# Retention scores cut to halves of 256 tokens, and a new order for the sampled states and the recurrence's chunks

## The chip, the core and the metric

The kernel runs on one core of one Trainium2 chip. The metric is the device time of one execution in microseconds (us). Engine names are those of the profile: PE is TensorE (PEld its weight loads), DVE is VectorE, ACT is ScalarE, POOL is GpSimd, and SP is the engine that mostly issues DMAs. Every engine works through its own instructions in a fixed order, and waits at the first one whose inputs are not there.

## What is computed

One layer of a decoder for a prompt of 512 tokens (D_MODEL 1024) and, beside it, for 8 sampled sequences of one token that continue from stored states. One input projection feeds two branches, retention (4 heads, key width 256, value width 512) and RWKV-7 (16 heads of 64). Both are gated, projected down, merged, projected out, and followed by a gated per-layer embedding and a final norm. The part that the change rewrites is the retention of one head:

```python
def chunk(s, qkv):
    qc, kc, vc = qkv
    inner = jnp.einsum('bhid,bhjd->bhij', qc, kc) * dmask
    o = jnp.einsum('bhij,bhjv->bhiv', inner, vc) + jnp.einsum('bhid,bhdv->bhiv', qc * q_dec, s)
    s = chunk_dec * s + jnp.einsum('bhjd,bhjv->bhdv', kc * k_dec, vc)
    return s, o
```

`dmask` is the decay to the power of the distance, lower triangular. The result does not depend on how long a chunk is: with one chunk of 512 there is no state term, with two of 256 the second half takes the first half's state. The outputs are the rows of both sets, the new retention and RWKV states of both, and the last normalised rows.

## The kernel before

All large products are made in a split form: an operand is written as a high part (a rounded copy, made by ACT) and a low part (the rest, made by DVE), and three matmuls stand for one. A weight block of 512 KB is fetched by SP into one of three `raw` buffers, ACT makes `whi` (line 147), DVE makes `wlo` (line 148), and PE runs the matmuls of line 160 on 128 x 128 weights with 256 or 264 columns of tokens (tokens 0 to 255, and 256 to 519, the last 8 of these being the sampled tokens). One projection of 128 output channels is 48 such matmuls.

The order of the instructions on each engine is made by a planner that simulates the program with a cost model and gives each engine the ready instruction of highest priority. Program order is the priority, `tc.high_priority(offset=n)` moves a block ahead of later code, and `tc.issue_after(x)` places the block's instructions on x's own engine behind x. `after(i, prior)` adds a real wait between two engines.

The stages, with their place in the profiled execution:

1. 0 to about 270 us: norm, transposes, and the inputs of RWKV (keys, receptances, values, gates), written to DRAM in the layout of the recurrence.
2. About 270 to 710 us: the loop over 4 heads of retention. Each head makes k and q (`rope`), then v in four blocks `j` of 256 input channels (line 838), the scores `sc` (line 863), the sampled sequences (`sampled(h)`: 4 MB of states in four tiles `tS` of 1 MB, loaded by POOL at line 758, decayed by ACT at line 764, updated by DVE at line 765, read by PE at line 770, stored by POOL at line 774), four gate projections, the outputs `o` (line 910), the new state `st` (line 921) and the transposes `ot` (line 928). The scores of key tile `jt` cover all later tokens: 512, 384, 256 and 128 columns, six matmuls each. The outputs of token tile `it` take 3(it+1) matmuls of 512 columns. Beside this DVE works off a triangular solve for RWKV and the sampled RWKV states in portions (`advance`).
3. About 700 to 900 us: `fills()`, which is eight projections `gate(O_MB, m)` of 48 matmuls and then eight `down_a(m)` of 96 matmuls (the fills, 16 in all), and beside them the eight steps `chunk(c)` of the RWKV recurrence. A chunk is a chain: PE `UO` (64 small matmuls, line 1025), copies `R` on ACT and DVE, PE `U` (line 1034), copies into `SV`, PE `dS` (line 1040) and `UO` (line 1043), DVE the next `SV` (line 1049), ACT `Ot` (line 1056). The banks of UO are two, so the next chunk's UO also waits for `Ot`. After each second chunk follow `finish_rwkv` (DVE and ACT) and `emit_rwkv` (PE transposes `gt`, line 985, and DVE). The list `AT` says after how many fills each chunk stands in the program. All chunks have high priority, so that the planner may run them ahead of that place.
4. After the last chunk: `emit_rwkv` of the last pair, PE transposes `so` of the last state (line 1133), then the RWKV rows `yb` are loaded back (line 1149; the first load waits for the transposes), split into `ybhi` and `yblo` (lines 1150 and 1151), and projected by `w_down_b`. That projection is the next PE work behind the fills.
5. About 900 us to the end: `w_down_b`, `w_out`, the embedding and the output.

Of the kernel before, what the change touches and what calls it, by code (L numbers as in the profile page):

```python
# [41 lines left out]
def constants():  # L42
    import numpy as np

    f = np.float32
    c = {}
    inv = (10000.0 ** (-np.arange(128) / 128)).astype(f)
    pos = np.concatenate([np.arange(T), np.full(B8, 4096)]).astype(f)
    ang = (pos[:, None] * inv[None, :]).astype(f)
    c["cos"] = np.ascontiguousarray(np.cos(ang).T.astype(f))  # L50
    c["sin"] = np.ascontiguousarray(np.sin(ang).T.astype(f))
    j = np.arange(128)[:, None]
    i = np.arange(T)[None, :]
    c["dmask"] = np.stack([np.where(i >= j, GAM[h] ** np.maximum(i - j, 0) / 16.0, 0.0) for h in range(H)], 1).astype(f)
    jj = np.arange(T).reshape(4, 128).T
    c["kdec"] = np.stack([GAM[h] ** (511 - jj) / 16.0 for h in range(H)], 1).astype(f)
    s = np.arange(64)[:, None]
    t = np.arange(64)[None, :]
    le, lt = (s <= t).astype(f), (s < t).astype(f)
    ev = np.concatenate([np.concatenate([le, -0.5 * lt], 1), np.concatenate([le, lt], 1)], 0)  # L60
    od = np.concatenate([np.concatenate([-0.5 * lt, le], 1), np.concatenate([lt, le], 1)], 0)
    c["gmask"] = np.concatenate([ev, od, ev, od], 1)
    r = np.ones((128, NT), f)
    r[:, 0:T:C] = 0.0
    r[:, T:] = 0.0
    c["reset"] = r
    ind = np.zeros((128, NPAIR, 16), f)
    for p in range(NPAIR):
        ind[:64, p, 2 * p] = 1.0
        ind[64:, p, 2 * p + 1] = 1.0  # L70
    c["ind"] = ind
    c["indT"] = np.ascontiguousarray(np.concatenate([ind.transpose(2, 1, 0)] * 2, 0))
    bd = np.zeros((128, 128), f)
    bd[:64, :64] = 1.0
    bd[64:, 64:] = 1.0
    c["bdiag"] = bd
    return c


def body(tc, A, O, dbg=None, upto="Z"):  # L80
# [11 lines left out]
    with es:  # L92
# [516 lines left out]
        pB.tile([128, 1280], F32R, tag="ihi", name="ihi")  # L609
# [135 lines left out]
        dve.tensor_tensor(s8, s8, i4[:, 2], ALU.add)  # L745
        dve.tensor_tensor(sum8, s8, i4[:, 3], ALU.add)

        def sampled(h):
            qz = pR.tile([128, 2, 4, 34], F32, tag="qz", name="qz", bufs=1)
            dve.memset(qz, 0.0)  # L750
            dve.tensor_copy(qz[:, :, :, 0], qs[:, h, :, 0:4])
            dve.tensor_copy(qz[:, :, :, 33], qs[:, h, :, 4:8])
            po = pq.tile([128, 512], F32, tag="po", name="po")
            for g in range(2):
                Ss = []
                for i in range(2):
                    S = pT.tile([128, 4, NT], F32, tag="tS", name="tS", bufs=4)[:, :, 0:DV]
                    pool.dma_start(S, A["state_ret"][0, 4 * g:4 * g + 4, h, 128 * i:128 * i + 128, :].rearrange("b p v -> p b v"))
                    Ss.append(S)
                for b in range(4):  # L760
                    vb = bank("vb")
                    pe.matmul(vb, sel[:, 4 * g + b, :], vsr, start=True, stop=True)  # L762
                    for i, S in enumerate(Ss):
                        act.activation(S[:, b, :], S[:, b, :], AF.Copy, scale=GAM[h])  # L764
# [26 lines left out]
        OFF = [0, 512, 896, 1152]  # L791
        GBC = [0, 0, 0, 4, 8]
        for h in range(H):
            roped = {}
# [32 lines left out]
            for j in range(4):  # L827
                ready = fetch(w_in[256 * j:256 * j + 256, O_V + DV * h:O_V + DV * h + DV])
                raws, w = raws[-1:] + [wide(ready[0])], [wide(t) for t in weights(None, ready=ready)]
                if j % 2:  # L830
                    ms = [pe.matmul(vsm[32 * g:32 * g + 32], hst[:, 2 * j - 2 + g, :], raws[g // 2][:, g % 2, :],  # L831
                                    start=(j == 1), stop=(j == 3), skip_group_check=True) for g in range(4)]
                    side_by_side(ms)
                    after(ms[0], marks[2])
                for jt in range(4):
                    for k in range(2):
                        for x, (w_, r) in enumerate(((w[0], hhi), (w[0], hlo), (w[1], hhi))):
                            m_ = pe.matmul(vps[jt], r[:, 2 * j + k, 128 * jt:128 * jt + 128], w_[:, k, :],  # L838
                                           start=(j == 0 and k == 0 and x == 0), stop=(j == 3 and k == 1 and x == 2))
                tail[:] = [getattr(m_, "ins", m_)]  # L840
                advance("v")
            vhi = pB.tile([128, 4, DV], F32R, tag="vhi", name="vhi")
            vlo = pB.tile([128, 4, DV], F32R, tag="vlo", name="vlo")
# [7 lines left out]
            qhi, qlo, _ = roped["q"]  # L851
            khi, klo, kf = roped["k"]

            dmask = pB.tile([128, T], F32, tag="dmask", name="dmask", bufs=1)
            (sp if h else pool).dma_start(dmask, A["dmask"][:, h, :])
            ihi = pB.tile([128, 1280], F32R, tag="ihi", name="ihi")
            ilo = pB.tile([128, 1280], F32R, tag="ilo", name="ilo")
            for jt in range(4):
                n = T - 128 * jt
                ps = bank("sc")  # L860
                seq = [(i, a_, b_) for i in range(2) for a_, b_ in ((khi, qhi), (khi, qlo), (klo, qhi))]
                for x, (i, a_, b_) in enumerate(seq):
                    pe.matmul(ps[:, 0:n], a_[:, i, 128 * jt:128 * jt + 128], b_[:, i, 128 * jt:T],  # L863
                              start=(x == 0), stop=(x == 5))
                s_ = pB.tile([128, T], F32, tag="s_", name="s_", bufs=1)
                dve.tensor_tensor(s_[:, 0:n], ps[:, 0:n], dmask[:, 0:n], ALU.mult)
# [12 lines left out]
            for jt in range(4):  # L879
# [5 lines left out]
            po = sampled(h)  # L885

            gs = []
            for i in range(4):
                g = pB.tile([128, NT], F32, tag="vg", name="gs", bufs=4)
                for (j, c0, c1), ps in zip(HV, proj(w_in[:, col(O_GA + DV * h, i)], hhi, hlo)):  # L890
                    act.activation(g[:, c0:c1], ps, AF.Silu)
                act.activation(gs8[:, 4 * h + i, :], g[:, T:NT], AF.Copy)
                gs.append(g)
                advance("gate")
                if h == H - 1 and i == 2:
                    ya_tiles(h, pT)
# [7 lines left out]
            ot = [x[:, i, :] for x in (pB.tile([128, 2, DV], F32, tag=t, name="ot") for t in ("qhi", "qlo")) for i in range(2)]  # L904
            for it in range(4):
# [5 lines left out]
                o = ot[it]  # L911
                act.activation(o, ps, AF.Square, accum_out=oss[:, it:it + 1])
                act.activation(o, ps, AF.Copy)
            rsqrt(ort, oss, 1.0 / DV, NORM_EPS)
            for it in range(4):
                act.activation(ot[it], ot[it], AF.Copy, scale=ort[:, it:it + 1])
            for i in range(2):
                ps = bank("st")
                seq = [(jt, a_, b_) for jt in range(4) for a_, b_ in ((dhi, vhi), (dhi, vlo), (dlo, vhi))]
                for x, (jt, a_, b_) in enumerate(seq):  # L920
                    pe.matmul(ps, a_[:, jt, 128 * i:128 * i + 128], b_[:, jt, :], start=(x == 0), stop=(x == 11))  # L921
# [408 lines left out]
```

## Time and profile before

| | |
|---|---|
| median of 3 runs | 1075.98 us (1072.61 to 1078.3) |
| profiled execution | 1071.51 us, its span 1069.7 us |
| PE / PEld busy | 1042.0 / 974.8 us |
| DVE / ACT / POOL busy | 785.2 / 494.8 / 79.5 us |
| mean granted PE clock | 0.992 |
| moved by DMA | 199.45 MB, mean 186 GB/s |

The span runs from the first to the last instruction. Matmuls overlap in their pipeline and their ends are modelled: the duration of one is longer than its distance to the next, and a PE that is shown busy is not a PE at its peak. A wait row names who waited, for whom, the total, the number of times and the longest.

### The profile page before, as it was taken

The page shows a single profiled execution, that of the slowest core. Times are in us where ns is not written, and L with a number is a line of the kernel's source. Part 1 is how long each engine was busy: PE and PEld are TensorE (multiplying, and loading weights), DVE is VectorE, ACT ScalarE, POOL GpSimd, SP SyncE. Part 2 cuts the span into 40 slices and gives each one's busy share as a digit, 9 for nine tenths or more (in the row PEclk, how much of TensorE's full clock was granted, in tenths as well). Part 3 has the DMA queues.
Part 4 walks back from the last instruction along what each step waited for, and adds up shares of the span by engine and source line. Part 5 has one row for each costly group of instructions (what it writes and reads, how often), then busy time and mean ns, then how long its engine had stood idle before and what let it go on. Part 6 is the DMA issues. An engine that isn't in the chain of part 4 may idle for free.

```text
span 1069.7 us, 22049 instructions
## 1 busy us (share of the span) xinstructions
PE 1042.0 (97%) x8932; PEld 974.8 (91%) x8932; DVE 785.2 (73%) x1429; ACT 494.8 (46%) x973; POOL 79.5 (7%) x139
## 2 busy tenths in 40 slices
PE   7999999999999999999999999998999999999995
PEld 6999989999879788987989889898999999999995
DVE  6647989884499699949894698864777755666875
ACT  6744565544464543373445333354323224334554
POOL 2000110100300200010010000110001100000000
PEclk8999999999999999999999999999999999999998
DMA  5623488788943943493288633969996649643222
GB/s 182 179 80 99 122 191 223 188 246 228 330 160 90 327 146 99 144 319 103 86 310 229 230 115 112 328 198 330 309 283 214 171 145 302 206 119 100 81 59 81
DMA packets 239224, 199.45 MB, mean 186 GB/s; under 512 B 58988, under 2 KB 203225, under 8 KB 237970
## 3 DMA queue, kind: packets, MB, share of 16 engines
q1 hardware_dynamic: 225586, 149.60, 47.7%
q0 software_dynamic: 13376, 48.17, 13.2%
q8 instruction: 70, 1.15, 0.4%
q14 instruction: 32, 0.26, 0.1%
q10 hardware_dynamic: 160, 0.27, 0.1%
HBM read 137.70 MB, written 60.00 MB: 185 GB/s over the span
## 4 chain that ended last, share of the span: by engine, by line
PE 85%; DMA 6%; DVE 3%; ACT 2%; issue 1%; SPq 1%; POOL 0%; DVEq 0%; POOLq 0%; ACTq 0%
PE ph L160 58%; PE phv L838 8%; PE o L910 3%; PE st L921 2%; PE sc L863 1%; PE po L770 1%; PE g L506 1%; PE UO L1025 1%; DMA raw<-in_w_ple_gate_dram 1%; DMA raw<-in_w_in_dram 1%; DMA yalo<-YAd 1%; DMA BKt<-BKd 1%; DMA MBd<-mg 1%; PE vb L762 1%; PE vsm L831 1%
## 5 line engine op out<-in xcount | busy, mean ns | idle before, releaser
L160 PE MATMUL ph<-hhi,whi 128*128 128x256 f32 (+2 forms) x1296 | 370.5, 286 | 0.9 <-ACT hhi L282 0.4
L160 PE MATMUL ph<-hlo,whi 128*128 128x256 f32 (+2 forms) x1296 | 369.4, 285 | 0.2 <-DVE hlo L283 0.2
L160 PE MATMUL ph<-hhi,wlo 128*128 128x256 f32 (+2 forms) x1296 | 368.8, 285 | 0.5 <-DVE wlo L148 0.5
L160 PEld LDWEIGHTS ph<-hhi,whi 128*128 128x128 f32 x1296 | 244.2, 189 | 6.1 <-issue 1.7
L160 PEld LDWEIGHTS ph<-hhi,wlo 128*128 128x128 f32 x1296 | 245.0, 189 | 2.2 <-DVE wlo L148 0.7
L160 PEld LDWEIGHTS ph<-hlo,whi 128*128 128x128 f32 x1296 | 244.5, 189 | 1.9 <-DVE hlo L283 0.7
L147 ACT ACTIVATE whi<-raw 128x1024 fp32r<-128x1024 f32 x135 | 142.9, 1059 | 208.9 <-PE ph L160 154.2
L148 DVE TENSOR_TENSOR wlo<-raw,whi 128x1024 fp32r<-128x1024 f32 x135 | 164.8, 1221 | 86.4 <-ACT whi L147 85.4
L160 PE MATMUL ph<-yalo,whi 128*128 128x256 f32 (+1 forms) x256 | 72.4, 285 | 0.0
L160 PE MATMUL ph<-yahi,whi 128*128 128x256 f32 (+1 forms) x256 | 72.2, 284 | 0.0
L160 PE MATMUL ph<-yahi,wlo 128*128 128x256 f32 (+1 forms) x256 | 71.9, 285 | 0.0
L623 DVE TENSOR_TENSOR tm<-M 128x62 f32<-128x62 f32 (+30 forms) x62 | 52.9, 853 | 0.6
L625 DVE TENSOR_TENSOR M<-M,tm 128x62 f32<-128x62 f32 (+30 forms) x62 | 52.8, 852 | 0.6
L838 PE MATMUL phv<-whi,hhi 128*128 128x512 f32 x128 | 51.5, 403 | 0.0
L838 PE MATMUL phv<-whi,hlo 128*128 128x512 f32 x128 | 50.5, 395 | 0.0
L160 PEld LDWEIGHTS ph<-yalo,whi 128*128 128x128 f32 x256 | 48.1, 188 | 0.3
L160 PEld LDWEIGHTS ph<-yahi,whi 128*128 128x128 f32 x256 | 48.1, 188 | 0.2
L160 PEld LDWEIGHTS ph<-yahi,wlo 128*128 128x128 f32 x256 | 47.8, 188 | 0.3
L838 PE MATMUL phv<-wlo,hhi 128*128 128x512 f32 x128 | 46.8, 395 | 0.5 <-DVE wlo L148 0.5
L765 DVE SCALAR_TENSOR_TENSOR tS<-vb,ks,tS 128x512 f32<-128x512 f32 x64 | 44.1, 742 | 3.3 <-PE vb L762 3.3
L764 ACT ACTIVATE tS<-tS 128x512 f32<-128x512 f32 x64 | 35.0, 620 | 12.5 <-DMA tS<-in_state_ret_dram 12.4
L215 ACT ACTIVATE mg<-ph 128x256 f32<-128x256 f32 (+1 forms) x48 | 17.7, 378 | 41.2 <-PE ph L160 20.6
(454 smaller groups left out, 2120.0 us busy)
## 6 DMA issues: line engine op xcount, KB each, us to landing
raw<-in_w_in_dram SPq DMA_DIRECT2D x97, 512.0 KB, 5.0
tS<-in_state_ret_dram POOLq DMA_DIRECT2D x16, 1024.0 KB, 8.4
out_dram<-tS POOLq DMA_DIRECT2D x16, 1024.0 KB, 9.9
KR<-KRd SPq DMA_DIRECT2D x8, 1024.0 KB, 9.5
raw<-in_w_down_a_dram SPq DMA_DIRECT2D x16, 512.0 KB, 6.8
KRd<-KRS SPq DMA_DIRECT2D x16, 256.0 KB, 4.5
KRd<-GM SPq DMA_DIRECT2D x16, 256.0 KB, 4.8
BKt<-BKd SPq DMA_DIRECT2D x8, 512.0 KB, 9.9
```

Of the source, the lines that this page charges most:

```text
L147: cp = act.activation(hi, raw, AF.Copy)
L148: sb = dve.tensor_tensor(lo, raw, hi, ALU.subtract)
L160: m_ = pe.matmul(ps[:, 0:c1 - c0], w[:, k, :], r[:, k0 + k, c0:c1], start=(x == 0), stop=(x == n_ - 1))
L215: act.activation(g[:, c0:c1], ps, fn, scale=scale)
L506: ms = [pe.matmul(gs[2 * q + hh][:, c * 128:(c + 1) * 128], BK[hs_, 4 * q + c, :], KRS[hs_, 4 * q + c, :], start=True, stop=True) for q in ...
L623: dve.tensor_tensor(tv, M[:, 0:s, s:s + 1].to_broadcast([128, s, n]), M[:, s:s + 1, s + 1:C].to_broadcast([128, s, n]), ALU.mult)
L625: dve.tensor_tensor(M[:, 0:s, s + 1:C], M[:, 0:s, s + 1:C], tv, ALU.add)
L764: act.activation(S[:, b, :], S[:, b, :], AF.Copy, scale=GAM[h])
L765: last = dve.scalar_tensor_tensor(S[:, b, :], vb, ks[:, h, i, 4 * g + b:4 * g + b + 1], S[:, b, :], ALU.mult, ALU.add)
L838: m_ = pe.matmul(vps[jt], r[:, 2 * j + k, 128 * jt:128 * jt + 128], w_[:, k, :], start=(j == 0 and k == 0 and x == 0), stop=(j == 3 and k ...
L910: pe.matmul(ps, a_[:, o_:o_ + 128], b_[:, jt, :], start=(x == 0), stop=(x == len(seq) - 1))
L921: pe.matmul(ps, a_[:, jt, 128 * i:128 * i + 128], b_[:, jt, :], start=(x == 0), stop=(x == 11))
```

## The change

Four edits are made together.

The scores are made within halves of 256 tokens: key tiles 0 to 3 cover 256, 128, 256 and 128 columns. The state of the first half is made from dhi and dlo (whose decay runs to token 511) and split into `shi` and `slo`; the outputs of token tiles 2 and 3 are the product of q with it (`oc`, six matmuls of 512 columns each), scaled per token by `qdec`, plus the scores of the second half. The state `st` at the end is then the second half's product plus `shi` plus `slo`, added by DVE.

The four loads of the sampled states of a head are issued in one go (`sampled_states`); in head 0 the first two wait for the last matmul of v's block 1, the other two for that of block 3 (`vmark`). The sampled work of head 0 moves behind the first gate projection.

In the recurrence, chunk c stands after 6, 8, 9, 10, 11, 12 and 13 fills for c = 1 to 7 (before: 3, 6, 8, 9, 11, 12 and 13), and its matmuls are now held behind the last matmul of those fills (`issue_after(tail[0])`).

```diff
+            SS = sampled_states(h)       # h == 0: after(ld, vmark[g]) on each load
+            if h:
+                po = sampled(h, SS)
...
-                n = T - 128 * jt
+                n = HT - 128 * (jt % 2)
...
+            vk = ((dhi, vhi), (dhi, vlo), (dlo, vhi))
+            shi = pB.tile([128, 2, DV], F32R, tag="shi", name="shi")
+            slo = [p_.tile([128, DV], F32R, tag=t, name="slo", bufs=1) for p_, t in ((pB, "vph"), (pR, "on"))]
+            for i in range(2):
+                ps = bank("st")
+                for x, (jt, (a_, b_)) in enumerate((jt, ab) for jt in range(2) for ab in vk):
+                    pe.matmul(ps, a_[:, jt, 128 * i:128 * i + 128], b_[:, jt, :], start=(x == 0), stop=(x == 5))
+                act.activation(shi[:, i, :], ps, AF.Copy)
+                dve.tensor_tensor(slo[i], ps, shi[:, i, :], ALU.subtract)
...
-                seq = [(jt, a_, b_) for jt in range(it + 1) for a_, b_ in ((ihi, vhi), (ihi, vlo), (ilo, vhi))]
+                seq = [(jt, a_, b_) for jt in range(it // 2 * 2, it + 1) for a_, b_ in ((ihi, vhi), (ihi, vlo), (ilo, vhi))]
...
+            ot = [pB.tile([128, NT], F32, tag="ro_k", name="ot", bufs=2)[:, 0:DV] for _ in range(2)]
...
+            for it in (2, 3):
+                ps = bank("oc")
+                seq = [(i, a_, b_) for i in range(2) for a_, b_ in ((qhi, shi[:, i, :]), (qhi, slo[i]), (qlo, shi[:, i, :]))]
+                for x, (i, a_, b_) in enumerate(seq):
+                    pe.matmul(ps, a_[:, i, 128 * it:128 * it + 128], b_, start=(x == 0), stop=(x == 5))
+                pss.append(ps)
...
+            for it in (2, 3):
+                act.activation(ot[it], pss[it - 2], AF.Copy, scale=qdec[:, h, it - 2:it - 1])
+            for it in (2, 3):
+                dve.tensor_tensor(ot[it], ot[it], within(it), ALU.add)
+                sqo = pB.tile([128, NT], F32, tag="ro_q", name="sqo", bufs=1)
+                act.activation(sqo[:, 0:DV], ot[it], AF.Square, accum_out=oss[:, it:it + 1])
...
-                act.activation(st, ps, AF.Copy)
+                dve.tensor_tensor(st, ps, shi[:, i, :], ALU.add)
+                dve.tensor_tensor(st, st, slo[i], ALU.add)
...
-        AT = [0, 3, 6, 8, 9, 11, 12, 13, 16]
+        AT = [0, 6, 8, 9, 10, 11, 12, 13, 16]
         for c in range(NCH):
-            with tc.high_priority(offset=20000):
+            with ExitStack() as cs_:
+                if c:
+                    cs_.enter_context(tc.issue_after(tail[0]))
+                cs_.enter_context(tc.high_priority(offset=20000))
                 PS = chunk(c)
```

More of the change, by code (lines that the diff above doesn't have):

```diff
@@ L55, in constants @@
     jj = np.arange(T).reshape(4, 128).T
+    c["qdec"] = np.stack([GAM[h] ** (np.arange(-255.0, 1.0).reshape(2, 128).T) for h in range(H)], 1).astype(f)
     c["kdec"] = np.stack([GAM[h] ** (511 - jj) / 16.0 for h in range(H)], 1).astype(f)
@@ L608, in body @@
         pB.tile([128, 4, DV], F32R, tag="vlo", name="vlo")
-        pB.tile([128, 1280], F32R, tag="ihi", name="ihi")
+        pB.tile([128, 768], F32R, tag="ihi", name="ihi")
         cos = pB.tile([128, NT], F32, tag="cos", name="cos")
@@ L746, in body, with sampled_states, sampled @@
         dve.tensor_tensor(sum8, s8, i4[:, 3], ALU.add)
-        def sampled(h):
+        def sampled_states(h):
+            Ss = []
+            for g in range(2):
+                for i in range(2):
+                    S = pT.tile([128, 4, NT], F32, tag="tS", name="tS", bufs=4)[:, :, 0:DV]
+                    ld = pool.dma_start(S, A["state_ret"][0, 4 * g:4 * g + 4, h, 128 * i:128 * i + 128, :].rearrange("b p v -> p b v"))
+                    if h == 0:
+                        after(ld, vmark[g])
+                    Ss.append(S)
+            return Ss
+        def sampled(h, SS):
             qz = pR.tile([128, 2, 4, 34], F32, tag="qz", name="qz", bufs=1)
@@ L754, in sampled @@
             for g in range(2):
[L755 to L759, printed above, removed]
+                Ss = SS[2 * g:2 * g + 2]
                 for b in range(4):
@@ L789, in sampled_out @@
                               gs8[:, hs_, :].rearrange("p i (g b) -> p i b g", g=2), ALU.mult)
-        OFF = [0, 512, 896, 1152]
+        vmark = []
+        OFF = [0, 256, 384, 640]
+        qdec = pB.tile([128, H, 2], F32, tag="qdec", name="qdec")
+        pool.dma_start(qdec, A["qdec"])
         GBC = [0, 0, 0, 4, 8]
@@ L852, in body @@
             khi, klo, kf = roped["k"]
[L854 to L857, printed above, removed]
+            dmask = pB.tile([128, HT], F32, tag="dmask", name="dmask", bufs=1)
+            (sp if h else pool).dma_start(dmask, A["dmask"][:, h, 0:HT])
+            ihi = pB.tile([128, 768], F32R, tag="ihi", name="ihi")
+            ilo = pB.tile([128, 768], F32R, tag="ilo", name="ilo")
             for jt in range(4):
-                n = T - 128 * jt
+                n = HT - 128 * (jt % 2)
                 ps = bank("sc")
@@ L891, in body @@
                     act.activation(g[:, c0:c1], ps, AF.Silu)
-                act.activation(gs8[:, 4 * h + i, :], g[:, T:NT], AF.Copy)
+                a_ = act.activation(gs8[:, 4 * h + i, :], g[:, T:NT], AF.Copy)
                 gs.append(g)
+                if h == 0 and i == 0:
+                    with tc.issue_after(getattr(a_, "ins", a_)):
+                        po = sampled(h, SS)
                 advance("gate")
@@ L903, in body, with within @@
             ort = pB.tile([128, 4], F32, tag="ort", name="ort", bufs=2)
-            ot = [x[:, i, :] for x in (pB.tile([128, 2, DV], F32, tag=t, name="ot") for t in ("qhi", "qlo")) for i in range(2)]
-            for it in range(4):
+            vk = ((dhi, vhi), (dhi, vlo), (dlo, vhi))
+            shi = pB.tile([128, 2, DV], F32R, tag="shi", name="shi")
+            slo = [p_.tile([128, DV], F32R, tag=t, name="slo", bufs=1) for p_, t in ((pB, "vph"), (pR, "on"))]
+            for i in range(2):
+                ps = bank("st")
[3 more added lines that the diff above has]
+                dve.tensor_tensor(slo[i], ps, shi[:, i, :], ALU.subtract)
+            def within(it):
                 ps = bank("o")
-                seq = [(jt, a_, b_) for jt in range(it + 1) for a_, b_ in ((ihi, vhi), (ihi, vlo), (ilo, vhi))]
+                seq = [(jt, a_, b_) for jt in range(it // 2 * 2, it + 1) for a_, b_ in ((ihi, vhi), (ihi, vlo), (ilo, vhi))]
                 for x, (jt, a_, b_) in enumerate(seq):
@@ L910, in body @@
                     pe.matmul(ps, a_[:, o_:o_ + 128], b_[:, jt, :], start=(x == 0), stop=(x == len(seq) - 1))
-                o = ot[it]
-                act.activation(o, ps, AF.Square, accum_out=oss[:, it:it + 1])
-                act.activation(o, ps, AF.Copy)
+                return ps
+            ot = [pB.tile([128, NT], F32, tag="ro_k", name="ot", bufs=2)[:, 0:DV] for _ in range(2)]
+            for it in range(2):
+                ps = within(it)
+                act.activation(ot[it], ps, AF.Square, accum_out=oss[:, it:it + 1])
+                act.activation(ot[it], ps, AF.Copy)
+            pss = []
+            for it in (2, 3):
[4 more added lines that the diff above has]
+                pss.append(ps)
+            ot += [pB.tile([128, 2, DV], F32, tag=t, name="ot")[:, 0, :] for t in ("qhi", "qlo")]
+            for it in (2, 3):
[4 more added lines that the diff above has]
+                act.activation(sqo[:, 0:DV], ot[it], AF.Square, accum_out=oss[:, it:it + 1])
             rsqrt(ort, oss, 1.0 / DV, NORM_EPS)
```

10 lines of the change are left out of this document (5 added, 5 removed).

## The prediction

> **What bounds the kernel now.** I read the page's busy shares and chain first, then the waits of PE, then PE's clock around each pause, and last the chain behind the last chunk of the recurrence.
>
> ```profile
> span 1069.7 us, 22049 instructions
> PE 1042.0 (97%) x8932; PEld 974.8 (91%) x8932; DVE 785.2 (73%) x1429; ACT 494.8 (46%) x973; POOL 79.5 (7%) x139
> ...
> PE 85%; DMA 6%; DVE 3%; ACT 2%; issue 1%; SPq 1%; POOL 0%; DVEq 0%; POOLq 0%; ACTq 0%
> ```
>
> PE is the bound: 97% busy and 85% of the chain that ended last. So only two things shorten the run: fewer or narrower matmuls, and pauses of PE taken away. Work moved between DVE, ACT and the queues counts only if PE comes to wait for it. In the two stages that the change touches, PE's waits are few:
>
> ```profile
> PE UO L1025 <- ACT Ot L1056: 3.4, 3, 2.7
> PE vsm L831 <- issue: 2.6, 1, 2.6
> PE phv L838 <- DVE wlo L148: 0.5, 1, 0.5
> ACT tS L764 <- DMA tS<-in_state_ret_dram: 3.6, 1, 3.6
> ```
>
> From the timeline of POOL, and windows (length, then PE, PEld, DVE, ACT and POOL busy, PE clock, DMA share, GB/s):
>
> ```profile
> 284.30 0.76 POOL L758 DMA_DIRECT2D tS<-in_state_ret_dram  x1
> ```
>
> ```profile
> 292.00:296.00 4.00, 1.36 (x11) 0.24 (x9) 2.04 (x4) 4.00 (x8) 0.00 (x0) 1.00 1.02 399
> 296.00:300.00 4.00, 4.00 (x21) 3.25 (x18) 3.93 (x9) 4.00 (x10) 0.00 (x0) 1.00 1.02 374
> 297.00:309.00 12.00, 12.00 (x54) 9.82 (x53) 11.90 (x21) 7.80 (x15) 0.00 (x0) 1.00 0.38 131
> 734.00:738.00 4.00, 1.27 (x36) 1.14 (x36) 3.80 (x6) 2.88 (x7) 0.00 (x0) 0.97 1.07 377
> 738.00:742.00 4.00, 4.00 (x68) 3.78 (x68) 3.67 (x8) 4.00 (x10) 0.00 (x0) 0.60 1.00 321
> ```
>
> Two pauses stand out. In 292 to 296 PE has 1.36 us of work in 4, in head 0's v: the DMA engines are full (share 1.02) because the 4 MB of sampled states were sent for at 284.3, so v's next block came late. ACT stood 3.6 us at a `tS` that had not landed. In 734 to 738 PE has 1.27 us: chunk 1's UO was placed straight behind chunk 0 and waited for ACT's `Ot` to free its banks. The clock granted afterwards was 1.00 in the first case and 0.60 over 4 us in the second, so this pause cost more than its length.
>
> **The change part by part.** Durations are of the profiled execution (1071.5 us with 1.8 us around its span). The median of the runs shown lies 4.5 us above it (0.4%). I add the sum to both.
>
> *Narrower scores.* Widths 512, 384, 256, 128 become 256, 128, 256, 128, with the count of matmuls the same.
>
> ```profile
> L863 PE MATMUL sc<-qhi,klo 128*128 128x512 f32 x8 | 3.2, 395 | 0.0
> L863 PE MATMUL sc<-qhi,klo 128*128 128x384 f32 x8 | 2.7, 338 | 0.0
> L863 PE MATMUL sc<-qhi,klo 128*128 128x256 f32 x8 | 2.2, 281 | 0.0
> L863 PE MATMUL sc<-qhi,klo 128*128 128x128 f32 x8 | 2.2, 275 | 0.0
> ```
>
> Four heads make 24 matmuls of each kind: 24 x (395 - 281) = 2.7 us and 24 x (338 - 275) = 1.5 us, together 4.2 us less. The 128-column row is hardly cheaper than the 256-column one, so I don't scale by columns. The Trainium skill, "TensorE: Matmul & The Clock Gate", section "Wait — 56ns, not 53.3ns?", says that back-to-back matmuls are spaced by columns over 2.4 GHz plus about 2.5 ns; by that the saving would be 24 x 107 ns twice, 5.1 us. The outputs cost nothing on PE: 30 matmuls of 512 columns per head before (3+6+9+12), 18 within halves plus 12 `oc` after; the state has 24 both times.
>
> *The other engines in the heads' tails.*
>
> ```profile
> L869 DVE TENSOR_TENSOR ilo<-s__4119,ihi x1: 682/682/682, 321.2 to 321.2; 128x512 fp32r<-128x512 f32 x1
> L869 DVE TENSOR_TENSOR ilo<-s__4130,ihi x1: 550/550/550, 323.9 to 323.9; 128x384 fp32r<-128x384 f32 x1
> L869 DVE TENSOR_TENSOR ilo<-s__4141,ihi x1: 414/414/414, 328.2 to 328.2; 128x256 fp32r<-128x256 f32 x1
> L869 DVE TENSOR_TENSOR ilo<-s__4152,ihi x1: 285/285/285, 331.8 to 331.8; 128x128 fp32r<-128x128 f32 x1
> ```
>
> ```profile
> 355.00:385.00 30.00, 30.00 (x203) 25.88 (x202) 18.79 (x46) 22.40 (x46) 4.87 (x7) 1.00 0.85 299
> 685.00:712.00 27.00, 27.00 (x179) 24.70 (x177) 18.61 (x48) 16.85 (x35) 4.86 (x7) 1.00 0.65 211
> ```
>
> Per head DVE gains eight passes over 512 columns (two for `slo`, two adds into `ot`, four for `st`): 8 x 0.68 = 5.4 us. It loses 0.27 + 0.26 us twice, in the mask and the `ilo` passes (taking the mask's like `ilo`'s): net about 4.4 us. ACT swaps two copies of `st` for two of `shi`, and copy and square stay two per token tile: nothing. The tail's windows (first and last head) have DVE busy 18.8 of 30 and 18.6 of 27 us, so 4.4 us fits. A new chain stands there: state product, ACT copy, DVE subtract, `oc`, ACT scale, DVE add, square, reciprocal root, transposes. Half of the state matmuls that stood behind the outputs now stand ahead of them, so less of the head's own work covers the root. What covers it is the next head's k and q projections, whose k rotation now waits for `ot` (it lies in its buffers), or in the last head the gates. All rows of these windows show PE full, so I take 0.5 us for four tails, bounds 0 and 4 (one pause of 1 us each, under the 2.7 us seen elsewhere).
>
> *Sampled states.* With the loads of head 0 behind v's blocks 1 and 3 (about 297 and 309 us), the DMA engines are free when v's blocks 1 to 3 are fetched. The 2.6 us and the 0.5 us just ahead go: 3.1 us. Late next would be the gates' weights, but the window from 297 to 309 has a DMA share of 0.38, which has room for 2 MB at each mark. On POOL nothing of head 0 stands behind these waiting loads that is needed before them, since `dmask` goes out ahead. Bounds: 0 (the pause moves) to 3.6 (a clock loss, too). The order of loads and stores in later heads I take at nothing; PE has no wait there.
>
> *Chunks behind their fills.* Chunk 1 now has six fills between itself and the start. Its wait goes: 2.7 us, plus 4 us x (1 - 0.60) = 1.6 us of clock, plus the other 0.7 us of the row's 3.4: 5.0 us less, bounds 2.7 and 5.0. But chunk 7 must now wait for fill 13. Where it stood, from the chain, from two windows that count line 160 alone, and from the timelines of SP, ACT, DVE and PE:
>
> ```profile
> 838.98 2.02 PE UO L1025 x64
> ...
> 852.51 16.38 PE ph L160 x135
> ```
>
> ```profile
> 838.90:880.40 41.50, 34.86 (x279) 33.67 (x279) 1.00 0.60 167
> 838.90:896.60 57.70, 51.06 (x413) 49.83 (x412) 1.00 0.66 183
> ```
>
> ```profile
> L1133 PE MATMUL so<-ident,PS x8: 271/272/273, 876.4 to 880.3; 128*64 128x128 f32 x8
> ```
>
> ```profile
> 884.63 0.37 SPq L142 DMA_DIRECT2D raw<-in_w_down_b_dram  x1
> 885.22 0.41 SPq L1149 DMA_DIRECT2D yb<-YBd  x1
> ...
> 890.11 1.06 ACT L1150 ACTIVATE ybhi<-yb 128x1024 fp32r<-128x1024 f32 x1 [3.80 <-DMA yb<-YBd]
> 892.54 1.06 ACT L1150 ACTIVATE ybhi<-yb 128x1024 fp32r<-128x1024 f32 x1 [0.30 <-DMA yb<-YBd]
> 893.64 1.23 DVE L1151 TENSOR_TENSOR yblo<-yb,ybhi 128x1024 fp32r<-128x1024 f32 x1
> 896.97 0.37 PE L160 MATMUL ph<-ybhi,whi 128*128 128x256 f32 x1
> ```
>
> From chunk 7's UO to the end of the fills PE ran 413 fill matmuls; behind fill 13 (eight gates and five `down_a`) only three `down_a` are left, 3 x 96 = 288. At 16.38/135 = 0.121 us each, PE has 15.1 us less to do while chunk 7's chain runs. That chain needed 41.5 us up to the last `so` at 880.4, with 279 fill matmuls between its steps. Then came the `yb` loads, which SP issued late, behind a weight fetch that waited until 884.6; the first half of the rows was split at 893.64 + 1.23 = 894.9, and PE took it up at 896.97. After the change 288 - 279 = 9 matmuls (1.1 us) are left behind `so`. The loads can go at once, since the fetch ahead of them is then early: 0.3 us, 0.45 to the second load, 5.5 us to its split (887.0 to 892.5), 1.06 and 1.23 us: 8.5 us. So PE stands 8.5 - 1.1 = 7.4 us. Bounds: 13.4 us if SP stays in the way as before (894.9 - 880.4 - 1.1), and 0 if the planner packs the chain closer. I take 7.4, since the fetch that held SP follows the fills, not the chain. A pause that long lowers the clock; by the only row that shows it, another 1.6 us. The Trainium skill, "TensorE: Matmul & The Clock Gate", section "What's actually happening", says that one idle window of about 3.4 us halves the clock until another such window is busy; that would be 1.7 us here. The trace agrees in part: a pause of 2.7 us was followed by 4 us at 0.60, one of 2.6 us by 1.00.
>
> *Sum.* -4.2 - 3.1 - 5.0 + 7.4 + 1.6 + 0.5 = -2.8 us: 1068.7 us for the profiled execution, 1073.2 on the median. I give 1073.
>
> **The rivals.**
>
> *The end is covered after all.* If chunk 7's chain needs 9 us less, the pause of 7.4 + 1.6 us is gone and the sum is -11.8: 1064. For it: gaps of the chain were filled with fill matmuls that the planner chose by its own clock, and PE could have run `U`, `dS` and `so` earlier. Against it: the planner's clock is the same after the change, and 279 of the 288 are used up by the same gaps.
>
> *Slower: the late chunk 7 decides alone.* If the `yb` loads stay where they were, the pause is 13.4 + 1.6 us, and the sum is -4.2 - 3.1 - 5.0 + 15.0 + 0.5 = +3.2: 1079. It turns into a loss from a pause of 10.7 us (12.3 of gains less 1.6). With four tails of 1 us it is 1083. For it: the gap at the end in the trace is 14.5 us. Against it: SP's wait.
>
> *The change doesn't do what it says for head 0.* The 4 MB moved behind v meet the gates' weights, and the pause comes back there: 3.1 us less gain, 1076. Against it: the DMA share of 0.38.
>
> **How the numbers follow.** About 0.5%, or 5.4 us, is what a measurement of this kernel can tell from no change: under 1070.6 is faster, over 1081.4 slower. The forecast has a chance of 0.47; its own range by the bounds (tails, pause 4 to 11) is 1068 to 1078, so some 0.13 of it counts as faster. The covered end has 0.30 (faster), the late chunk 0.16 (0.11 slower, 0.05 the same), head 0's pause 0.07 (the same, 0.02 slower). That gives faster 0.43, same 0.44, slower 0.13. From 1062 to 1082 lie at least 8 in 10 of it.
>
> **What would show it.** Score matmuls of 256 and 128 columns only, 48 of each width; no PE wait at `vsm`, and DMA share near 1 moved to behind 297; no wait of chunk 1 for `Ot`; and a PE pause ahead of the first `ph<-ybhi`, with a clock under 1 behind it. If that pause is missing the time is near 1064. A PE wait at `oc` or `ot` in the tails would make the 0.5 us wrong, and a count other than 288 fill matmuls behind chunk 7 the whole end.

## The result, and the profile after

The changed kernel takes 1117.4 us (median of 4 runs, 1113.8 to 1118.7) where the kernel before takes 1076.0 us: a ratio of 1.038 (95% interval 1.034 to 1.042), 41 us slower. The forecast was 1073 us. Line numbers of the changed kernel are higher than those printed above by 1 to about 50; the names of tiles are the same.

From the page of the changed kernel (span, busy times, the chain that ended last):

```profile
span 1116.6 us, 22095 instructions
...
PE 1049.7 (94%) x8932; PEld 977.5 (88%) x8932; DVE 800.2 (72%) x1461; ACT 491.9 (44%) x973; POOL 80.2 (7%) x140
...
PE 82%; DVE 7%; DMA 5%; ACT 3%; issue 2%; POOL 0%; SPq 0%; DVEq 0%; POOLq 0%; ACTq 0%
```

The span grew by 46.9 us. PE idle (span less busy time) went from 27.7 to 66.9 us, which is 39.2 of them; the other 7.7 us are added busy time, with the mean granted clock at 0.976 where it was 0.992. PE's waits of the changed kernel name the places (total, times, longest):

```profile
PE yas L793 <- ACT on L790: 20.4, 3, 8.7
PE ph L161 <- ACT ybhi L1199: 11.7, 1, 11.7
PE vsm L842 <- ACT whi L148: 4.4, 3, 1.9
...
PE phv L849 <- ACT whi L148: 2.8, 1, 2.8
```

These four rows alone are 39.3 us. Three belong to the heads: `yas` are the transposes of the sampled output, and `vsm` and `phv` are v. The second is the pause ahead of `w_down_b`.

Windows of the changed kernel around the step from head 0 to head 1 (PE, PEld, DVE, ACT, POOL busy, PE clock, DMA share, GB/s), and two of the kernel before:

```profile
380.00:390.00 10.00, 10.00 (x73) 9.37 (x72) 8.18 (x22) 7.93 (x15) 0.56 (x1) 1.00 0.19 74
390.00:400.00 10.00, 10.00 (x51) 8.14 (x50) 9.64 (x16) 2.21 (x5) 0.56 (x1) 1.00 0.29 107
400.00:410.00 10.00, 7.83 (x34) 6.00 (x32) 10.00 (x18) 1.46 (x4) 0.00 (x0) 1.00 0.07 26
410.00:420.00 10.00, 3.50 (x15) 1.51 (x15) 7.30 (x16) 2.06 (x5) 0.00 (x0) 0.58 0.00 1
```

```profile
360.00:370.00 10.00, 10.00 (x54) 6.78 (x53) 1.83 (x5) 7.62 (x17) 0.76 (x1) 1.00 0.93 335
390.00:400.00 10.00, 10.00 (x48) 7.17 (x47) 10.00 (x13) 2.48 (x6) 0.00 (x0) 1.00 0.37 107
```

In the kernel before DVE was nearly idle just ahead of the roots (1.83 of 10 us) and full once v of the next head ran (10.00). After the change PE stops in that full stretch. What DVE did there, as first and last instruction of the sampled output's root, from DVE's timeline of the kernel before:

```profile
371.93 0.15 DVE L178 TENSOR_SCALAR nv<-os 128x1 f32<-128x1 f32 x1
...
377.54 0.16 DVE L186 SCALAR_TENSOR_TENSOR os<-nt,os 128x1 f32<-128x1 f32 x1
```

and of the changed kernel, with some of what lies between:

```profile
389.15 0.68 DVE L969 TENSOR_TENSOR st<-st,slo 128x512 f32<-128x512 f32 x1
...
391.94 0.15 DVE L179 TENSOR_SCALAR nv<-os 128x1 f32<-128x1 f32 x1
...
407.19 1.18 DVE L624 TENSOR_TENSOR tm<-M 128x986 f32<-128x986 f32 x1
408.28 0.16 DVE L186 TENSOR_TENSOR nt<-nt,nv 128x1 f32<-128x1 f32 x1
...
415.50 0.15 DVE L187 SCALAR_TENSOR_TENSOR os<-nt,os 128x1 f32<-128x1 f32 x1
```

The same 13 instructions of 0.15 us took 5.6 us before and 23.6 us after: on an engine with a fixed order nearly each stood behind long ones (a solve instruction, a rotation, a split or a gate product). In heads 1 to 3 they took 2.1 us each before, and 23.7, 25.3 and 10.4 us after. The root of the four outputs, just ahead of them, was hardly stretched: it took 2.2 us before, and 2.7 to 4.7 us in the four heads after. Its first and last instruction in head 0 of the changed kernel:

```profile
381.91 0.16 DVE L179 TENSOR_SCALAR nv<-oss 128x4 f32<-128x4 f32 x1
...
384.61 0.16 DVE L187 SCALAR_TENSOR_TENSOR ort<-nt,ort 128x4 f32<-128x4 f32 x1
```

The 13 start late because the sampled root's input is written into the tile `on` (ACT, 390.47 us), which slo[1] also uses, and slo[1] is read last by the addition at 389.15. On ACT and PE, changed kernel:

```profile
390.47 0.59 ACT L788 ACTIVATE on<-po 128x512 f32<-128x512 f32 x1
...
415.75 0.69 ACT L790 ACTIVATE on<-po,os 128x512 f32<-128x512 f32 x1 [3.48 <-DVE os L187]
```

```profile
416.50 1.11 PE L793 MATMUL yas<-ident,on 128*128 128x128 f32 x4 [8.67 <-ACT on L790]
417.54 1.94 PE L842 MATMUL vsm<-raw,hst 128*32 128x512 f32 x8
```

`vsm` needs the PSUM bank of `po`, which is free only when `on` is made. In the kernel before `on` was made at 377.73 us and `vsm` came at 391.62 us. `vsm` also reads the fetched weights themselves, so their buffer is free only behind it. On SP, which also stores the late outputs, the fetches of v's next blocks follow; the kernel before and the changed kernel:

```profile
378.33 5.37 SPq L934 DMA_DIRECT2D YAd<-gs  x4
392.71 31.76 SPq L142 DMA_DIRECT2D raw<-in_w_in_dram  x7
```

```profile
393.79 7.93 SPq L980 DMA_DIRECT2D YAd<-gs  x4
419.54 9.42 SPq L143 DMA_DIRECT2D raw<-in_w_in_dram  x5
```

The next block of v is sent for 27 us later than before.

At the end of the recurrence, changed kernel: PE's line of projections from chunk 7 to the last fill, then the windows behind it, SP, and ACT:

```profile
884.00:926.70 42.70, 36.06 (x290) 34.83 (x288) 1.00 0.53 156
```

```profile
926.70:938.70 12.00, 0.32 (x4) 0.10 (x2) 4.31 (x7) 4.43 (x5) 0.19 (x1) 0.66 0.99 272
938.70:945.00 6.30, 5.62 (x28) 5.33 (x29) 2.51 (x3) 1.43 (x3) 0.00 (x0) 0.57 0.96 325
```

```profile
925.86 0.38 SPq L143 DMA_DIRECT2D raw<-in_w_down_b_dram  x1
...
929.86 5.90 SPq L1198 DMA_DIRECT2D yb<-YBd  x4
```

```profile
935.89 1.06 ACT L1199 ACTIVATE ybhi<-yb 128x1024 fp32r<-128x1024 f32 x1 [3.44 <-DMA yb<-YBd]
```

The last `so` started at 924.9 us; the loads of `yb` went out 5.0 us later, and the first of the four landed 6.0 us after that with the DMA engines full (share 0.99). PE stood 11.7 us, and the clock of the next 6.3 us was 0.57 in the mean.

### The profile page after: what moved, and what is told of

Read it like the earlier page. It is cut to its first block, busy times and chain, and to the rows that moved or that the text cites. A ratio compares the mean times of both kernels' runs of the same rounds, so it can differ in the third digit from the quotient of the medians.

```text
span 1116.6 us, 22095 instructions
## 1 busy us (share of the span) xinstructions
PE 1049.7 (94%) x8932; PEld 977.5 (88%) x8932; DVE 800.2 (72%) x1461; ACT 491.9 (44%) x973; POOL 80.2 (7%) x140
## 4 chain that ended last, share of the span: by engine, by line
PE 82%; DVE 7%; DMA 5%; ACT 3%; issue 2%; POOL 0%; SPq 0%; DVEq 0%; POOLq 0%; ACTq 0%
PE ph L161 60%; PE phv L849 5%; DMA raw<-in_w_in_dram 3%; PE o L938 2%; PE po L778 1%; PE g L507 1%; PE UO L1071 1%; DMA raw<-in_w_ple_gate_dram 1%; PE st L966 1%; PE st L929 1%; PE oc L951 1%; PE vsm L842 1%; ACT whi L148 1%; PE U L1080 1%; PE dS L1086 1%
## 5 line engine op out<-in xcount | busy, mean ns | idle before, releaser
L161 PE MATMUL ph<-yahi,whi 128*128 128x264 f32 (+1 forms) x256 | 73.1, 286 | 0.0
L161 PE MATMUL ph<-yalo,whi 128*128 128x264 f32 (+1 forms) x256 | 72.9, 285 | 0.0
L161 PE MATMUL ph<-ybhi,whi 128*128 128x264 f32 (+1 forms) x128 | 37.5, 293 | 11.7 <-ACT ybhi L1199 11.7
```

What stands on the lines that cost most here:

```text
L161: m_ = pe.matmul(ps[:, 0:c1 - c0], w[:, k, :], r[:, k0 + k, c0:c1], start=(x == 0), stop=(x == n_ - 1))
```

## Experiments

Each kernel was timed in turns with the kernel before; ratios are to it, with 95% intervals.

| kernel | us | ratio | PE idle, us |
|---|---|---|---|
| only the sampled states | 1076.6 | 1.001 (0.998 to 1.004) | 28.1 |
| only the dealing of the chunks | 1089.3 | 1.014 (1.010 to 1.018) | 40.1 |
| only the scores within halves | 1105.0 | 1.028 (1.024 to 1.032) | 58.6 |
| all (the change) | 1117.4 | 1.038 (1.034 to 1.042) | 66.9 |
| all, slo[1] in another tile | 1101.5 | 1.026 (1.021 to 1.030) | 52.0 |

### The parts alone, and slo[1] out of the shared tile

Only the scores within halves (sampled states and chunks as before):

> The kernel before with only the scores within halves (slo[1] in the tile `on`, as in the change); sampled states and chunks as before. Theory A (shared tile) and theory B (DVE load): the loss is here, the head loop ends 40 us or more later than before, and the time is 1105 to 1120 us. Theory C (sampled states): 1070 to 1076 us, that is the kernel before less the 4.2 us of narrower scores.

Measured 1105.0 us. PE waits 14.8 us at `yas`, so the loss in the heads belongs to this part. Behind chunk 7 stand 307 fill matmuls, although the dealing is the old one, and PE waits 8.6 us for `ybhi`.

Only the sampled states:

> The kernel before with only the loads of the sampled states issued in one go (in head 0 behind v's blocks 1 and 3) and head 0's sampled work behind its first gate. Theories A and B: 1071 to 1077 us, with the pause of 2.6 us in head 0's v gone. Theory C: over 1100 us, with PE waiting for the sampled output or for v's weights.

Measured 1076.6 us: no difference. The pause in head 0's v is gone (the window that had 1.36 of 4 us is full), but a wait has come in the chunks:

```profile
292.00:296.00 4.00, 4.00 (x22) 2.35 (x21) 4.00 (x8) 0.69 (x3) 0.00 (x0) 1.00 0.23 45
...
815.00:825.00 10.00, 7.58 (x97) 7.20 (x96) 6.42 (x9) 2.13 (x3) 0.88 (x1) 0.83 0.82 246
```

Only the dealing of the chunks:

> The kernel before with only the chunks of the recurrence placed behind 6, 8, 9, 10, 11, 12 and 13 fills and held there. All of theories A to C leave the heads alone here. My sum for this part: chunk 1's wait gone (5.0 us less), a pause ahead of the first product of w_down_b with its clock (9.0 us more): 1080 us. Rival, the pause is as long as in the changed kernel (11.7 us and a clock of 0.66 for part of the next stage) and the gain at chunk 1 does not come, since other steps of the chain wait instead: 1084 to 1092 us. Rival, the pause belongs to the late heads alone: 1071 us.

Measured 1089.3 us: the first rival. PE's waits of this kernel, and ACT at the place of chunk 1's old wait:

```profile
PE ph L160 <- ACT ybhi L1153: 11.5, 1, 11.5
PE ph L160 <- ACT mg L215: 3.9, 1, 3.9
```

```profile
736.87 2.19 ACT L646 ACTIVATE yahi<-yalo 128x512 fp32r<-128x512 f32 x4 [5.71 <-DMA yalo<-YAd]
738.96 0.57 ACT L1056 ACTIVATE Ot<-UO 64x512 f32<-64x512 f32 x1
...
740.04 1.18 ACT L215 ACTIVATE mg<-ph 128x256 f32<-128x256 f32 x4
```

Chunk 1 no longer stands there, and PE stops all the same: now it is the fill that waits for a bank. ACT stood 5.71 us at a split whose load had not landed, and `Ot` and `mg` were queued behind it. The kernel before has the same row, which I had not read:

```profile
735.12 2.19 ACT L646 ACTIVATE yahi<-yalo 128x512 fp32r<-128x512 f32 x4 [5.35 <-DMA yalo<-YAd]
```

The change with slo[1] in another tile:

```diff
-            dmask = pB.tile([128, HT], F32, tag="dmask", name="dmask", bufs=1)
+            dmask = pB.tile([128, T], F32, tag="dmask", name="dmask", bufs=1)[:, 0:HT]
-            slo = [p_.tile([128, DV], F32R, tag=t, name="slo", bufs=1) for p_, t in ((pB, "vph"), (pR, "on"))]
+            slo = [pB.tile([128, DV], F32R, tag=t, name="slo", bufs=1) for t in ("vph", "dmask")]
```

> The changed kernel with one tile moved: the second half of slo (slo[1]) lies in the tile of dmask (made 512 columns wide again) and no longer in the tile `on`, which the sampled sequences' output also uses. Theory A, the shared tile: after the change sampled_out of a head can write `on` only when the last addition into st has read slo[1]; its chain of small DVE instructions then falls into the next head's v, where PE stands at its transposes (yas, three waits, 20.4 us) and then runs at a lower clock. The whole loss up to the end of the head loop, 43.5 us, should go, and the time comes to 1072 to 1082 us. Theory B, load: the eight added DVE passes of 512 columns a head (5.4 us a head) fill DVE beside the solve, wherever the tile lies; the time then stays above 1105 us and the waits at yas stay or move to oc and ot. Theory C, the order of the sampled states: the waits come from the loads or from head 0's later place; the time stays above 1105 us too, and the kernel with that edit alone shows it.

Measured 1101.5 us. Theory A holds for 16 us and no more: the wait at `yas` falls from 20.4 to 3.5 us, and the sampled root takes 8.1 us (399.12 to 407.24) instead of 23.6, but now the outputs' root ahead of it takes 18.4 us (380.70 to 399.05). In head 1 the sampled root still takes 24.0 us, and in heads 2 and 3 no root takes over 4.4 us. Less the 14 us that the chunks cost alone, the heads still lose about 12 us, and the gain of the scores is missing.

### What holds the heads up

Outputs out of the rotation's buffers; the same with the old dealing:

> The kernel with slo[1] in dmask's tile (the first experiment, 1101.5 us, with the new dealing of the chunks in it), and now also with the four outputs ot in the tiles qhi and qlo, as in the kernel before, so that none of them lies in ro_k; the square's throw-away output goes to the PSUM bank it was read from and no longer to ro_q. Theory D, the rotation's buffers: with ot in ro_k (and the square in ro_q) the next head's rotation of k and q, and with it its scores, wait until the late outputs have been transposed; the trace of the first experiment has khi of head 1 only at 408 us, ahead of a pause of 3.6 us before the first scores. Without that the 11 us that the heads still lose there go: 1086 to 1092 us, and the chunks' part stays. Theory B, load: the DVE passes themselves are the price: 1099 to 1104 us.

> The same kernel with the chunks of the recurrence dealt as before. Of the change it keeps the scores within halves and the sampled states. Theory D and my term for the narrower scores (4.2 us less, nothing else): 1070 to 1075 us, no slower than the kernel before. Theory B: 1084 to 1090 us. If the parts do not add up, since the heads' pauses fall into the chunks' stage, it lies between.

Measured 1105.5 us (1.028, 1.024 to 1.032) and 1105.8 us (1.027, 1.023 to 1.031). Theory D falls: the first `khi` of head 1 comes at 397 us instead of 403 to 408, and PE waits all the same:

```profile
PE yas L793 <- ACT on L790: 8.2, 1, 8.2
...
PE yas L793 <- DVE st L967: 4.8, 1, 4.8
```

The sampled output moved ahead of the first half's state: in the change, with slo[1] in the other tile, and that with the old dealing and later splits:

```diff
+            sampled_out(h, po)
             oss = pB.tile([128, 4], F32, tag="oss", name="oss", bufs=2)
...
-            sampled_out(h, po)
```

> The changed kernel with one call moved: sampled_out(h) stands right behind the gates, ahead of the first half's state, and no longer behind the transposes ot. The tile `on` is still shared, but now slo[1] takes it over from the sampled output. Theory G, the bank: vsm of the next head needs the PSUM bank of po, which the sampled output holds until ACT has made `on`; in the kernel before that was at 377.7 us and vsm came at 391.6, in the first experiment `on` came at 407.4 and in the changed kernel at 415.8. The outputs now end some 10 us later (377 us instead of 367 in head 0), the roots behind them fall into the next head's v, where DVE is full, and their small instructions go one by one between long ones; whatever stands behind them holds vsm and v. With the sampled output ahead of all that, the waits at yas and vsm go, shared tile or not: 1086 to 1096 us (the chunks' part, 14 us, stays). Theory A, sharing as such: the first state now waits for the sampled output instead, and the time stays above 1105 us.

> The first experiment (slo[1] in dmask's tile, 1101.5 us) with the same call moved. Theory G: the 11 us that the heads still lost go: 1086 to 1092 us, all of it more than before in the chunks' part. Theory B, the eight DVE passes: DVE is as full as it was, other instructions come late in the place of these, and the time is 1098 to 1104 us.

> The same kernel with the chunks dealt as before and the splits of the loaded heads two fills later (which alone gave 3 us). Theory G with all gains: 4 us from the scores and 3 us from the splits: 1067 to 1072 us, faster than both kernels. Theory B: 1083 to 1088 us.

Measured 1130.1, 1128.3 and 1128.3 us (1.052, 1.051, 1.050; intervals within 0.005 of each): slower than the change itself. The waits at `yas` and `vsm` went, as theory G had it (one of 4.6 us is left), but others took their place. In the first of the three the planner now ran the whole v of head 1 (373 to 410 us) ahead of head 0's transposes (415 to 421 us), and before the last head's transposes it had spent more fills: 773 fill matmuls were left, against 1096 in the kernel before. PE's waits of that kernel, and its ACT:

```profile
PE UO L1071 <- DMA KR<-KRd: 11.2, 1, 11.2
...
PE o L939 <- ACT ot L956: 8.6, 1, 8.6
```

```profile
618.01 1.06 ACT L148 ACTIVATE whi<-raw 128x1024 fp32r<-128x1024 f32 x1 [12.80 <-DMA raw<-in_w_in_dram]
...
619.24 1.26 ACT L956 ACTIVATE ot<-oc,qdec 128x512 f32<-128x512 f32 x2
```

Again ACT stood at a load, with the copy that PE needed behind it. A moved call moves everything else here, so this does not show what the bank costs by itself.

Fewer root instructions, fewer added passes, a lighter DVE, and the old dealing, each on the kernel with slo[1] in the other tile:

> The first experiment (slo[1] in dmask's tile, 1101.5 us) with one refinement step instead of three in the two reciprocal roots of each head, that of the outputs (ort) and that of the sampled output; two steps of three are left out of these. That is six small DVE instructions less in each chain. Theory H, small between long: the trace has the twelve instructions of ort from 389.5 to 399.1 us in head 0, each behind a solve instruction or a split of 1.2 us, where the kernel before needed some 5 us; this chain is what makes the transposes, the sampled output and vsm late. With half of it gone the heads end 4 to 8 us earlier: 1092 to 1098 us. Theory B, eight DVE passes of 512 columns: they are 5.4 us a head against under 2 us of busy time saved here: 1099 to 1103 us.

> The first experiment with the state st copied by ACT from its bank, as in the kernel before, and without the two DVE additions of shi and slo for each half; the first half's state is left out of st. That is four of the eight added DVE passes, 2.7 us a head, and the last readers of slo. Theory B: half of what is left of the heads' loss goes, 5 to 8 us: 1093 to 1097 us. Theory H: these passes lie behind the outputs and beside the roots, and the roots stay where they are: 1098 to 1103 us.

> The first experiment with every second step of the triangular solve left out (its DVE instructions of 1.2 us; the portions stay where they were dealt). DVE then has room in v, and the roots are no longer cut up. If DVE's fullness in the tails and in v is what makes the rest of the heads' loss (theories B and H share that), the pauses at yas, vsm and sc go, and the time is 1084 to 1091 us, what the chunks' part costs alone or less. If it stays above 1097 us, the order of the chain itself (state, oc, outputs, roots) is too long for the work that covers it, whatever DVE has to do beside.

> The first experiment with the chunks dealt as before. If the parts add up: 1101.5 less the 14 us that the new dealing cost alone, 1085 to 1090 us. If late heads by themselves make the chunks late against the fills, as the kernel with only the scores within halves shows it (307 fill matmuls behind chunk 7 with the old dealing, and a pause of 8.6 us), most of the end's loss stays: 1096 to 1102 us.

Measured: one refinement step 1089.1 us (1.013, 1.010 to 1.016); no additions into `st`, so that the first half is missing from the state, 1098.6 us (1.022, 1.019 to 1.026); every second solve step left out 1082.4 us (1.006, 1.004 to 1.008); old dealing 1101.1 us (1.024, 1.021 to 1.027). (The expectation of the first puts the outputs' root at 389.5 to 399.1 us; that is its second half, it begins at 380.70.)

Twelve small instructions a head, under 2 us of busy time, give back 12 us; four passes of 0.68 us give 3 us, which the intervals don't tell from nothing (the other four added passes were not taken away). So theory H fits best: not the load that the change adds to DVE, but the chain of small instructions that now lies in a full stretch. With half the solve gone the sampled root of head 0 needs 2.1 us, and no wait in the heads is over 1 us:

```profile
373.60 0.15 DVE L179 TENSOR_SCALAR nv<-os 128x1 f32<-128x1 f32 x1
...
375.71 0.16 DVE L187 SCALAR_TENSOR_TENSOR os<-nt,os 128x1 f32<-128x1 f32 x1
```

That kernel is 7 us faster than the dealing alone; as the lighter DVE was not tried without the halves, this doesn't show the gain of the scores by itself.

The old dealing gave nothing back, so the parts don't add up. PE's line of projections from the last head's last transpose to the end of the fills, in the kernel before and in this one:

```profile
706.60:896.60 190.00, 139.51 (x1096) 133.46 (x1096) 0.99 0.81 244
```

```profile
730.30:911.40 181.10, 129.89 (x1015) 123.73 (x1015) 0.99 0.79 240
```

81 fill matmuls, 9.8 us at 0.121 us, had already been used in the last head to cover its longer tail. The fills are one reserve for both places: what the heads take is missing behind chunk 7, where 307 are left and PE waits 8.4 us for `ybhi`. Late heads are not needed for that. All kernels with the halves, but for the three with the moved call, have 1006 to 1015 fill matmuls left behind the last head's transposes. That holds also for the one with half the solve, whose last of these transposes come at 708.5 us (706.3 us in the kernel before). So with the halves PE pauses at the end under either dealing.

One root for both outputs (one chain of five columns), that with the old dealing and the later splits, and with the earlier dealing and the later splits:

```diff
+            act.activation(on, po, AF.Square, accum_out=oss[:, 4:5])
...
-            rsqrt(os2[:, 1:2], os2[:, 0:1], 1.0 / DV, NORM_EPS)
-            act.activation(on, po, AF.Copy, scale=os2[:, 1:2])
+            act.activation(on, po, AF.Copy, scale=ort[:, 4:5])
```

> The first experiment (slo[1] in dmask's tile, 1101.5 us) with one chain of root instructions a head in the place of two: the sampled output's sum of squares goes into a fifth column beside the four of the outputs, and one reciprocal root is made of all five. Nothing is left out; each head issues 13 small DVE instructions less, about as many as with one refinement step. Theory H (small instructions behind long ones set when the transposes, the sampled output and vsm come): 1086 to 1092 us, as with one step (1089.1 us). Rival, the steps that were left out mattered in another way than by their number, the sampled root now also waits for the last outputs: 1096 to 1103 us.

> The same kernel with the chunks dealt as before and the splits of the loaded heads two fills later. Theory H and the end by lateness: the heads end nearly in time, so the old dealing finds its fills again; the pause ahead of w_down_b is under 3 us and the time is 1070 to 1077 us, about that of the kernel before, since the 4 us of the scores are spent on what is left of the waits. Rival, late heads whatever the roots: a pause of 8 us at the end and 1083 to 1092 us.

> The same again with the changed dealing one fill earlier (5, 7, 8, 9, 10, 11, 12, held), and the later splits. Theory F (384 fill matmuls behind chunk 7 cover its chain): no pause of over 3 us ahead of w_down_b: 1071 to 1078 us. Rival as above: 1083 us or more.

Measured 1095.1 us (1.017, 1.012 to 1.021), 1093.8 us (1.017, 1.014 to 1.020) and 1093.7 us (1.016, 1.013 to 1.020). The number of small instructions counts: 13 fewer give 6 us, half of what the shorter chain gave, though `on` is made at 399.08 us, as early as with one step (397.40). What PE waits for now, 9.0 us at `vsm` in two heads, are v's weights: on SP their fetch stands right behind the store of a late output, which waits for `ot`.

```profile
401.63 0.34 SPq L978 DMA_DIRECT2D YAd<-gs  x1
402.15 0.38 SPq L143 DMA_DIRECT2D raw<-in_w_in_dram  x1
```

Neither dealing ends without a pause (8.7 and 8.9 us, with 308 fill matmuls behind chunk 7), as the second rival had it: 1006 fill matmuls are left behind the heads, as few as with the longer roots.

### The end

The dealing one fill earlier, on the kernel before; the expectation's "except chunk 3" is a slip, all seven were moved:

> The kernel before with the chunks held behind their fills as in the change, but each from chunk 1 on (except chunk 3) one fill earlier in the list: 5, 7, 8, 9, 10, 11, 12. Theory F, the place of chunk 7: behind it stand then about 384 fill matmuls of 0.121 us and no longer 288, that is 11.6 us more cover; the pause of 11.6 us ahead of w_down_b and some 4 us of clock behind it go, and the time is 1073 to 1078 us. Rival, the chain behind chunk 7 takes what cover there is, since the planner packs it no closer: the pause stays over 5 us and the time over 1081 us.

Measured 1078.6 us (1.002, 1.000 to 1.004). From chunk 7 to the end of the fills, this kernel:

```profile
846.90:901.10 54.20, 47.56 (x385) 46.36 (x384) 1.00 0.65 186
```

384 matmuls, as theory F counted, and PE goes on to `ybhi` after 0.4 us. From 738.9 us on it still waits 3.5 us for `Ot`.

The later splits, on the kernel before:

> The kernel before with one edit: the splits of the first three heads' output (ya_loaded, which ACT makes from a tile loaded back from DRAM) stand two fills later. Theory E, ACT's queue: PE's pause at 735 us comes from ACT, which stood 5.35 us at the first of these splits until its load had landed, with the copies Ot and mg queued behind it; chunk 1's place has nothing to do with it. The pause (2.9 us, 0.6 us and about 1.6 us of clock) goes: 1069 to 1073 us. Rival, the DMA engines (share 1.05 there): the next fill's weights are as late, and PE pauses at them: 1074 to 1078 us.

Measured 1073.6 us (0.998, 0.996 to 1.000). PE is busy all through the place of the old pause with the DMA engines as full as they were:

```profile
725.00:735.00 10.00, 10.00 (x153) 9.58 (x152) 2.61 (x3) 2.52 (x4) 0.00 (x0) 1.00 1.04 349
735.00:745.00 10.00, 10.00 (x175) 9.53 (x175) 7.29 (x11) 7.70 (x16) 0.00 (x0) 1.00 1.09 368
```

So ACT's queue made that pause, not the DMA engines alone. The last fill ends 4.4 us earlier, and a pause of 2.0 us ahead of `w_down_b`, with a clock of 0.83 from 895 to 905 us, takes a part back. It is the fastest kernel of this study, by a margin that the interval hardly tells from nothing.

## Why the prediction was wrong

*The other engines in the heads' tails*, 0.5 us with bounds 0 and 4, is the step that failed. Alone it cost about 30 us, the pause behind the fills that comes with it included. The load was right (DVE busy grew by 15.0 us, 17.6 were counted), but I judged it by its share of windows of 30 us, which mixed an idle stretch with a full one, and which ended at 385 us, just ahead of the stretch of head 0 that DVE fills to 10.00 of 10. The last square of the outputs came about 12 us later in head 0 (368.95 and 380.76 us), and behind it the 13 small instructions of the sampled root, held back further by the tile `on`, slid from the idle stretch into the full one. What hung on them was the sampled output and v of the next head, by the bank of `po` and by SP, where the stores of the outputs stand ahead of v's fetches: none of them stood in my list of who waits. The waiter that I did name, the rotation of k behind `ot`, was not the cause (theory D falls), and my sign for the tails, a PE wait at `oc` or `ot`, stayed away while PE waited at `yas`.

Beside the new dealing, which takes 1089.3 us alone, the other parts cost 28 us: 16 go with the shared tile (shown by moving slo[1]) and 12 with half of the small root instructions (shown by taking them away). These sizes hold beside that dealing only. Beside the old one the kernel with the shared tile and the one without it are 4 us apart (1105.0 and 1101.1 us; the first also has the old sampled states), which the intervals don't tell from nothing. How much comes over the bank and how much over SP stays open.

The Trainium skill, "VectorE: DVE Perf Modes", section "Rules for kernel authors", says of chained DVE operations that their number should be kept small. The runs agree (12 fewer a head gave 12 us, 13 fewer in another way 6 us), and the trace adds that it matters where they stand: 13 of them took 5.6 us in one place and 23.6 us in another.

*Sampled states*, -3.1 us: the pause went as said, the gain did not come (1.001). The lower bound of 0 was the value.

*Chunks behind their fills.* The 5.0 us of chunk 1 were not chunk 1's. The wait row named `Ot` on ACT; the row of ACT one step further named a load. With the chunks moved alone, the wait became 3.9 us of a fill; in the full change, where this stage comes later, 0.9 us of it is left at `UO`. The end pause was of the right kind, with 288 matmuls as counted, but mis-sized: 11.7 us and not 7.4, since SP issued the `yb` loads 5.0 us after the last `so` and not at once, with a weight fetch still ahead of them, and the first took 6.0 us to land. Of the clock I had 1.6 us; 6.3 us at 0.57 are 2.7 us. The Trainium skill, "TensorE: Matmul & The Clock Gate", section "What's actually happening", has one idle window of about 3.4 us halve the clock until another is busy. The trace agrees: in windows of 1 us the clock reads 0.50 from about 3.5 us into the pause until about 5.5 us behind its end.

*Narrower scores*, -4.2 us: the widths are as said, but no run shows their gain by itself.

The rival "late chunk 7 decides alone" (1079 to 1083 us) was the nearest in kind, and the dealing cost 14 us alone. None of the rivals had the heads as more than 4 us. One of the signs that I had named does tell: `vsm` was to have no wait, and has 4.4 us.

## What to carry to other kernels

When a change lengthens a chain on an engine with a fixed order, look at how full that engine is where the chain will land, not on average, and count the small dependent instructions, each of which can cost one long neighbour. Follow every tile, bank and queue that the late result holds to the next stage's first use of it, and a wait row one engine further back before its cost is called a gain. Work that covers one stage's tail is no longer there for the next.

## What was not expected of the hardware

A DVE instruction on one column (0.15 us busy) follows the one before it after about 0.2 us when nothing stands between (13 in 2.1 us). In PE's pause of 8.67 us of the changed kernel the clock goes to 0.50 about 3.8 us after PE's last work (407.8 us), and it is back at 1.00 about 5.4 us after PE has work again (416.5 us); in the one of 11.7 us the two are about 3.5 and 5.5 us.
